# The values of two attention stages as one seven-product form, in a two-layer encoder on one core

## The chip, the cores and the metric

The kernel runs on one core of a Trainium2 chip. A core has TensorE (PE) for matmuls, VectorE (DVE), ScalarE (ACT), GpSimd (POOL) and SyncE (SP), which here only issues loads. The metric is the device time of one execution in microseconds.

## The reference

Two layers, each with a half-step SwiGLU FFN, a mixer, an attention into 256 memory tokens and a second FFN, each followed by a layer norm; 512 tokens, width 1024, float32. The even layer's mixer is another one; the change touches the odd layer's mixer and the memory attention of both layers:

```python
def mixer_c(h, w_in, w_out, rpb):        # 16 heads of 64, grid of 8 rows x 64 columns
    q, k, v = jnp.split(h @ w_in, 3, axis=-1)
    ...
    s = jnp.einsum('bwhd,bawjhd->bhwaj', q_r, k_nb).astype(jnp.float32) * scale
    s = s + bias.astype(jnp.float32)[None]
    p = jax.nn.softmax(s.reshape(B, C_HEADS, GRID_W, kh * kw), axis=-1)
    ...
    return o @ w_out

def memory_attn(h, mem, w_q, w_kv, w_o): # 4 heads of 256
    q = (h @ w_q).reshape(B, S, MEM_HEADS, MEM_HEAD_DIM)
    k, v = jnp.split(mem @ w_kv, 2, axis=-1)
    ...
    p = jax.nn.softmax(s, axis=-1).astype(v.dtype)
    o = jnp.einsum('bhsm,bmhd->bshd', p, v).reshape(B, S, D_MODEL)
    return o @ w_o
```

The values of the mixer are a product of 512 x 1024 by 1024 x 1024, those of a memory stage one of 256 x 1024 by 1024 x 1024.

## The kernel before

Every large product keeps float32 accuracy by splitting each operand into a high part (a ScalarE cast) and a low part (a VectorE subtraction, `split`, L380) and adding three matmuls, high x high, high x low, low x high (`mm3`, L391). The activations are held by features in `xh` and `xl`. The FFNs and output projections already use a seven-product form of 2 x 2 block matrices (seven block products in place of eight, paid with sums of blocks); queries, keys and values do not.

No engine order is written by hand. The program is recorded as a list of operations, all through one helper, so every row of the profile says L160. A planner (`plan`, L198) then simulates the engines with a table of costs. TensorE takes, of the operations that are ready, the one that stands first in the program; VectorE, ScalarE and GpSimd take the one with the earliest due time, worked out backwards from TensorE. The result is a fixed order for each engine. Tiles come from pools (L357): 27 `slab` buffers of 4 KB a partition, 14 `t2` of 2 KB, 2 `raw` of 8 KB, and eight PSUM banks under the tags `a`, `d` and `t`. A pool grants its buffers in the order in which the program asks, so a load on SP's queue waits until the slab it was given is free, and all loads behind it wait too.

The mixer (`mixer_c`, L1291) starts when the third FFN's layer norm ends, tile of 128 tokens by tile. It makes the values of heads 0 to 3 (group 0), the queries and keys of pair 0, the queries of pair 1 and the scores of pair 0 (`weights_of`). Then it loops over eight pairs of heads: keys of the next pair, transposes of this pair's weights (`turned`), queries two pairs on, scores of the next pair, `attend` of this pair. After `attend` of pairs 0 to 5 come two of the four token tiles of one further group of values, so that groups 1 to 3 are made inside the loop. A tile of values uses weights that stand as high and low side by side, so that a step is one matmul of 512 columns and one of 256. The pair's softmax (VectorE's reductions with the biases, ScalarE's exponentials and normalising) runs while TensorE does attend, values and keys. The biases of a pair are two table loads and six sums on GpSimd.

A memory stage (`memory`, L1484) loops over four heads; `project` makes for each the keys and two blocks of queries, and at heads 0 and 2 the values of two heads, 48 matmuls of 512, with keys and values of the 256 memory tokens. In `todo` the values stand between the keys and the queries.

Of the kernel before, what the change touches and what calls it, by code (L numbers as in the profile page):

```python
# [20 lines left out]
P = 128  # L21
D = 1024
# [314 lines left out]
class Kernel:  # L337
# [80 lines left out]

    def w_cols_k(self, w, c0):
# [154 lines left out]
    def project(self, w, ps, lo, hi):  # L574

        for k in range(KB):
            self.mm3(ps[:, lo:hi], [z[:, k, :] for z in w], self.xT(k, lo, hi), k == 0, k == KB - 1)
# [327 lines left out]
    def ffn(self, i, ln_i, last, aside=None):  # L905
# [385 lines left out]
    def mixer_c(self, ln_i, last):  # L1291
# [3 lines left out]
        ends = [self.slab(F32R, (P, KB, P)) for _ in range(2)]  # L1295

        def values(grp, t):

            if t == 0:
                wv[0] = self.w_cols_side(w_in, 2 * D + 256 * grp)  # L1300
                vp[grp] = self.slab(F32, (P, 4, 256))
                if grp == 0:
                    for dst, lo in ((slice(64, 128), 0), (slice(0, 64), 448)):
                        nc.scalar.copy(ends[0][:, :, dst], self.xh[:, :, lo : lo + 64])
                        nc.vector.tensor_copy(ends[1][:, :, dst], self.xl[:, :, lo : lo + 64])
            ps = self.ps("t" if grp else "a")
            for k in range(KB):
                x = self.xT(k, 64 + t * P, 64 + (t + 1) * P) if t < 3 else [z[:, k, :] for z in ends]
                self.side_step(ps, x, wv[0][k // 2][:, k % 2], k)
# [101 lines left out]
        def attend(pts, pair):  # L1411
            po = self.ps("d")
            for j in range(4):
                for s in range(2):
                    own = po[64 * s : 64 * s + 64]
                    dst = own[:, j * P : j * P + 256] if j < 3 else own.rearrange("p (c n) -> p c n", c=4)[:, 0:4:3]
                    c0 = 64 * (2 * (pair % 2) + s)
# [3 lines left out]
                        dst, vp[pair // 2][:, j, c0 : c0 + 64], mv, start=j == 0, stop=j == 3, skip_group_check=True  # L1421
# [14 lines left out]
        vp, qs, ks, acts = {}, {}, {}, []  # L1436
        wv, wq, wk, wo = [None], [None], [None], {}
        for t in range(NT):
            values(0, t)
# [3 lines left out]
        us = weights_of(0)  # L1443
        for pair in range(8):
# [9 lines left out]
            else:  # L1454
                steps(5 if pair == 6 else 3)
            if pair < 7:
                us = weights_of(pair + 1)
# [6 lines left out]
            if pair < 6:  # L1464
# [246 lines left out]
```

## Time and profile before

| | before |
|---|---|
| median of 3 runs | 2096.86 us (2096.57 to 2097.29) |
| profiled execution | 2095.62 us |
| its span | 2093.8 us |
| POOL busy | 307.9 us (15%) |
| first memory stage: last two key pairs and the values of heads 0, 1 | 541.69 to 553.37 us of the span |
| last output matmul of the third FFN, start of the mixer | 1363.8 us |
| scores of pairs 0, 1 and 2 of the mixer | 1399.40, 1413.97, 1435.89 us |
| DMA | 276.99 MB, mean 132 GB/s |

The page gives for each engine its busy time. For a kernel whose first engine is nearly always busy the useful question is what else is waited for, and where; that is read from the timeline of this engine, whose rows end with what ended an idle time before them, if there was one.

### The profile page before, as it was taken

How to read it: one execution, taken by the hardware profiler on the slowest of the kernel's cores; microseconds unless marked ns; L12 is line 12 of the kernel's file. 1: busy time of each engine (PE TensorE's matmuls, PEld its weight loads, DVE VectorE, ACT ScalarE, POOL GpSimd, SP SyncE). 2: the span in 40 equal slices, each digit the busy share in tenths (PEclk: the TensorE clock that was granted, in tenths of full speed). 3: DMA queues.
4: the chain of work that ended last, by engine and by line, in shares of the span. 5: the costliest groups of instructions: out<-in, count | busy, mean ns of one | idle time of the engine just before them, and what ended most of it. 6: DMA issues, size and time to landing. Idle time of an engine off the chain costs nothing.

```text
span 2093.8 us, 33128 instructions
## 1 busy us (share of the span) xinstructions
PE 2078.1 (99%) x13044; PEld 1845.2 (88%) x13044; DVE 1752.3 (84%) x2515; ACT 1146.7 (55%) x1847; POOL 307.9 (15%) x389
## 2 busy tenths in 40 slices
PE   9999999999999999999999999999999999999997
PEld 7999988777888999998899999888878889999996
DVE  7789988788748979999889999854487488799996
ACT  5555543697545744555555455446565466455552
POOL 0001005310002010000300100412131020001002
PEclk9999999999999999999999999999999999999999
DMA  7566572004343467565545657332234434556651
GB/s 209 154 158 146 139 199 86 21 21 141 122 131 101 135 144 204 142 161 143 170 114 149 158 144 201 91 106 76 100 93 141 144 98 141 130 146 170 153 148 61
DMA packets 214204, 276.99 MB, mean 132 GB/s; under 512 B 9376, under 2 KB 162592, under 8 KB 214048
## 3 DMA queue, kind: packets, MB, share of 16 engines
q1 hardware_dynamic: 177536, 217.99, 32.7%
q0 software_dynamic: 36224, 56.63, 15.5%
q8 instruction: 102, 1.67, 0.3%
q14 instruction: 54, 0.44, 0.1%
q10 hardware_dynamic: 288, 0.26, 0.0%
HBM read 272.75 MB, written 4.19 MB: 132 GB/s over the span
## 4 chain that ended last, share of the span: by engine, by line
PE 96%; DVE 2%; issue 1%; DMA 1%; ACT 0%; POOL 0%; DVEq 0%; ACTq 0%; POOLq 0%
PE a L160 53%; PE d L160 27%; PE t L160 16%; DVE slab L160 1%; DVE x L160 1%; DMA slab<-ffn_w_up 0%; DVE t L160 0%; ACT slab L160 0%; ACT t L160 0%; DMA raw<-x_t 0%; POOL rms8y L160 0%; POOL slab L160 0%; DVE xl L160 0%; DVE mn L160 0%; DVE rh L160 0%
## 5 line engine op out<-in xcount | busy, mean ns | idle before, releaser
L160 DVE TENSOR_TENSOR slab<-slab,slab 128x1024 fp32r<-128x1024 f32 (+2 forms) x617 | 734.8, 1213 | 49.0 <-ACT slab L160 42.1
L160 PE MATMUL a<-slab,slab 128*128 128x256 f32 (+3 forms) x2384 | 583.8, 317 | 0.1
L160 ACT CAST slab<-slab 128x1024 fp32r<-128x1024 f32 (+2 forms) x457 | 463.5, 1038 | 197.9 <-DVE slab L160 133.7
L160 PE MATMUL a<-raw,slab 128*128 128x256 f32 x2432 | 459.8, 283 | 0.0
L160 PEld LDWEIGHTS a<-slab,slab 128*128 128x128 f32 (+1 forms) x2384 | 415.0, 190 | 38.6 <-issue 3.6
L160 PE MATMUL a<-xh,slab 128*128 128x256 f32 (+2 forms) x2000 | 445.4, 312 | 0.2 <-ACT slab L160 0.2
L160 PEld LDWEIGHTS a<-raw,slab 128*128 128x128 f32 x2432 | 388.2, 191 | 6.2 <-ACT t L160 0.2
L160 PEld LDWEIGHTS a<-xh,slab 128*128 128x128 f32 x2000 | 333.9, 190 | 25.0 <-ACT slab L160 1.1
L160 PE MATMUL a<-xl,slab 128*128 128x256 f32 (+2 forms) x1000 | 311.8, 312 | 0.0
L160 PE MATMUL d<-slab,t 128*128 128x512 f32 x1104 | 278.9, 392 | 0.0
L160 PEld LDWEIGHTS d<-slab,t 128*128 128x128 f32 x1104 | 200.3, 189 | 36.9 <-ACT t L160 0.4
L160 PE MATMUL t<-slab,t 128*128 128x512 f32 x828 | 207.5, 392 | 0.5 <-DVE x L160 0.3
L160 PEld LDWEIGHTS a<-xl,slab 128*128 128x128 f32 x1000 | 190.4, 190 | 13.5 <-DVE xl L160 0.2
L160 PEld LDWEIGHTS t<-slab,t 128*128 128x128 f32 x828 | 150.2, 189 | 28.9 <-issue 0.7
L160 DVE TENSOR_TENSOR slab<-raw,slab 128x1024 fp32r<-128x1024 f32 (+2 forms) x144 | 158.9, 1127 | 16.5 <-ACT slab L160 16.4
L160 PE MATMUL d<-slab,slab 128*128 128x512 f32 (+3 forms) x736 | 163.3, 415 | 0.0
L160 PE MATMUL d<-xh,slab 128*128 128x256 f32 (+1 forms) x720 | 153.1, 306 | 0.0
L160 ACT CAST slab<-raw 128x1024 fp32r<-128x1024 f32 (+1 forms) x128 | 119.7, 968 | 29.3 <-DMA raw<-ab_w_in 9.6
L160 PEld LDWEIGHTS d<-slab,slab 128*128 128x128 f32 (+1 forms) x736 | 105.3, 170 | 34.3 <-issue 12.6
L160 DVE SCALAR_TENSOR_TENSOR x<-d,x 128x512 f32<-128x512 f32 x174 | 118.7, 685 | 15.8 <-PE d L160 14.0
L160 PEld LDWEIGHTS d<-xh,slab 128*128 128x128 f32 x720 | 117.1, 191 | 5.1
L160 ACT COPY t<-a 128x512 f32<-128x512 f32 (+1 forms) x112 | 62.0, 556 | 96.0 <-DVE a L160 59.4
(132 smaller groups left out, 2492.2 us busy)
## 6 DMA issues: line engine op xcount, KB each, us to landing
slab<-ffn_w_gate SPq DMA_DIRECT2D x95, 512.0 KB
slab<-ffn_w_up SPq DMA_DIRECT2D x95, 512.0 KB
slab<-ffn_w_down SPq DMA_DIRECT2D x80, 512.0 KB
slab<-ffn_w_down POOLq DMA_DIRECT2D x40, 512.0 KB, 6.4
raw<-mem_w_kv SPq DMA_DIRECT2D x16, 1024.0 KB
slab<-ffn_w_gate POOLq DMA_DIRECT2D x19, 512.0 KB, 6.1
slab<-ffn_w_up POOLq DMA_DIRECT2D x19, 512.0 KB, 6.0
raw<-mem_w_q SPq DMA_DIRECT2D x8, 1024.0 KB
```

Of the source, the lines that this page charges most:

```text
L160: op.call = lambda: fn(*args, **kw)
```

## The change

All values of the mixer become one product in seven-product form, with two token blocks of 256 (each as two tiles of 128), two halves of the contraction and two halves of the 1024 columns. With a, b, c, d the four 512 x 512 blocks of the weights (a over b on the left, c over d on the right), products 1 and 2 use a and b, product 6 uses a + c + d, product 5 c + d, product 7 a + c, product 4 d, and product 3 a + c + d + b. Products 1, 2 and 3 take the tokens' high and low parts as they are; products 6, 5, 7 and 4 take sums of token blocks, made on VectorE from a float32 copy of the normalised tokens, which the third FFN now keeps in the `raw` pool (`keep`). The sums c + d and a + c + d are made on VectorE, a + c (onto a second copy of a) and the addition of b by accumulating DMAs of GpSimd's queue.

All 14 steps (seven products, two halves of their contraction) are issued ahead of the pair loop, after the scores of pair 0; the loop has no values any more. As `raw` is taken, the first queries' and keys' weights come in four quarters into slabs (`w_pairs`). In a memory stage the same steps, with one block of 128 tokens, are drawn three, two, two, three, two and then all that are left at six points among the projections of heads 0 and 1; the memory tokens are loaded a second time in float32 for their sums.

In the whole program matmuls fall from 12916 to 12804, VectorE's TENSOR_TENSOR instructions rise from 1470 to 1508, plain loads from 408 to 428, and GpSimd's DMAs from 120 to 132.

```diff
+    def w_pairs(self, w, c0):
+        got = self.w_halves(w, c0)
+        return [[[z[i][:, :, b * P : b * P + P] for z in got] for i in range(2)] for b in range(2)]
...
+            st = [z[k // 4][:, k % 4] if isinstance(z, list) else z[:, k, :] for z in w]
+            self.mm3(ps[:, lo:hi], st, self.xT(k, lo, hi), k == 0, k == KB - 1)
...
-                ln.update({"gb": self.load_ln(ln_i), "last": last, "keep": i == 1})
+                ln.update({"gb": self.load_ln(ln_i), "last": last, "keep": i in (1, 2)})
...
-        ends = [self.slab(F32R, (P, KB, P)) for _ in range(2)]
-        def values(grp, t):
...
-            self.side_sum(vp[grp][:, t], ps)
+        def shifted(q, s):
...
+        def value_sums():
+            t1, t2, t3, t4 = (self.slab(F32, (P, 4, 256)) for _ in range(4))
+            for z, x, y, op in ((t1, (0, 0), (0, 1), ALU.subtract), (t2, (1, 1), t1, ALU.add), (t3, (0, 1), (1, 1), ALU.subtract), (t4, (1, 0), t2, ALU.subtract)):
...
+            tokens.update({5: t1, 6: t2, 7: t3, 4: t4})
+        def value_ends():
...
+        def value_prep(m):
+            if m == 6:
+                value_sums()
+            if m in tokens:
+                tokens[m] = self.wide(tokens[m])
+            if m == 3:
+                ends.extend(self.t2(F32R, (P, 4, P)) for _ in range(2))
+                value_ends()
+        def stationary(m, k, b):
+            if m == 1 or m == 2:
+                return self.xT(4 * (m == 2) + k, 64 + b * P, 64 + b * P + P)
+            if m == 3:
+                return self.xT(4 + k, 320, 448) if b == 0 else [z[:, k] for z in ends]
+            return [z[:, k, b * P : b * P + P] for z in tokens[m]]
+        def value_done(f, s, b, ps, less=None):
+            if not room[f, s]:
+                room[f, s].append(self.slab(F32, (P, 2, 512)))
+            dst = room[f, s][0][:, b]
+            if less is None:
+                nc.scalar.copy(dst, ps)
+            else:
+                self.mix(dst, ps, less, ALU.subtract)
...
-                wq[0] = self.w_cols(w_in, 128 * pair)
+                wq[0] = self.w_pairs(w_in, 128 * pair) if pair == 0 else self.w_cols(w_in, 128 * pair)
...
-                wk[0] = self.w_cols(w_in, D + 128 * pair)
+                wk[0] = self.w_pairs(w_in, D + 128 * pair) if pair == 0 else self.w_cols(w_in, D + 128 * pair)
...
-                        dst, vp[pair // 2][:, j, c0 : c0 + 64], mv, start=j == 0, stop=j == 3, skip_group_check=True
+                        dst, room[pair // 4, j // 2][0][:, j % 2, c0 : c0 + 64], mv, start=j == 0, stop=j == 3, skip_group_check=True
...
-        for t in range(NT):
-            values(0, t)
...
+        made = self.staged(self.value_steps(w_in, 2 * D, 2, value_prep, stationary, value_done))
...
         queries(0, True)
         keys(0, True)
         queries(1)
         us = weights_of(0)
+        some(99)
...
-            if pair < 6:
-                for t in range(2):
-                    values(pair // 2 + 1, 2 * (pair % 2) + t)
...
+    def value_steps(self, w, c0, blocks, ready, stationary, done):
...
+        chain = {1: ("d", 1), 2: ("d", 1), 6: ("a", 6), 7: ("a", 6), 4: ("a", 6), 5: ("d", 5), 3: ("d", 5)}
+        at = {"a": (0, 0), "b": (1, 0), "c": (0, 1), "d": (1, 1)}
...
+        def fetch(name, i):
+            z = self.slab(F32, (P, 2, 512))
+            nc.sync.dma_start(out=z, in_=part(name, i))
+            return z
+        def plus(z, name, i):
+            nc.gpsimd.dma_start(out=z, in_=part(name, i), accum_op=ALU.add)
+        def load(m, i):
+            for name in {1: "a", 2: "b", 6: "cd"}.get(m, ""):
+                raw[name, i] = fetch(name, i)
+            if m == 7:
+                raw["v", i] = fetch("a", i)
+                plus(raw["v", i], "c", i)
+        def prep(m, i):
+            if i == 0:
+                ready(m)
+            if m == 6:
+                self.mix(raw["c", i], raw["c", i], raw["d", i], ALU.add)
+                self.mix(raw["a", i], raw["a", i], raw["c", i], ALU.add)
+            right[m, i] = self.wide(raw[{1: "a", 2: "b", 6: "a", 5: "c", 7: "v", 4: "d", 3: "a"}[m], i])
+            if m == 6:
+                plus(raw["a", i], "b", i)
+        def product(m, i):
+            tag, c = chain[m]
+            for b in range(blocks):
...
+                for k in range(2):
+                    self.mm3(
+                        ps, stationary(m, 2 * i + k, b), [z[:, k] for z in right[m, i]], m == c and i == 0 and k == 0, i == 1 and k == 1,
+                        skip_group_check=True,
+                    )
+                if i == 0:
+                    continue
+                if m == 1:
+                    own["c12", b] = self.t2(F32)
+                    nc.scalar.copy(own["c12", b], ps)
+                elif m == 6:
+                    self.mix(ps, ps, own["c12", b], ALU.subtract)
+                    nc.scalar.copy(own["c12", b], ps)
+                elif m == 5:
+                    own["c22", b] = self.t2(F32)
+                    nc.scalar.copy(own["c22", b], ps)
+                elif m == 7:
+                    done(1, 1, b, ps, own["c22", b])
+                elif m == 3:
+                    done(0, 1, b, ps, own["c12", b])
+                else:
+                    done(int(m == 4), 0, b, ps)
...
+        return [tuple(bound(f, m, i) for f in (load, prep, product)) for m in (1, 2, 6, 5, 7, 4, 3) for i in range(2)]
...
+        def value_prep(m):
+            if m == 1:
+                for q in range(2):
+                    raw.append(self.slab(F32, (P, 4, MEM)))
+                    nc.sync.dma_start(out=raw[q], in_=a["mem_t"][512 * q : 512 * q + 512].rearrange("(k p) m -> p k m", p=P))
...
+            if m in sums:
+                y = self.slab(F32R, (P, 2, 4, P))
+                self.split(sums[m], y[:, 0], y[:, 1])
+                sums[m] = y
...
             def values():
-                wv = self.w_cols512(w_kv, D + 256 * head)
-                vs.extend(self.pair() for _ in range(2))
-                for m in range(2):
-                    ps = self.ps("a")
-                    for k in range(KB):
-                        self.mm3(ps, memT(k, m * P, (m + 1) * P), [z[:, k % 2, :] for z in wv[k // 2]], k == 0, k == KB - 1)
-                    for j, both in enumerate(vs):
-                        self.split(ps[:, j * 256 : j * 256 + 256], *(z[:, m * 256 : m * 256 + 256] for z in both))
+                for _ in range(rate.pop(0) if rate else 0):
+                    next(made, None)
...
-            return got, [keys] + [values] * (head % 2 == 0) + [lambda: queries(0), lambda: queries(1)]
+            return got, [keys, values, lambda: queries(0), values, lambda: queries(1), values]
...
+        rate = [3, 2, 2, 3, 2, 99]
+        made = self.staged(self.value_steps(w_kv, D, 1, value_prep, stationary, value_done))
...
-            acts += attend(p, now, hs[head] if head < 2 else None)
+            acts += attend(p, [z[:, head % 2].rearrange("p (o n) -> p (o n)", o=1) for z in room[head // 2]], hs[head] if head < 2 else None)
```

How this moves the instructions, at three places. In the pair loop, TensorE before, where `attend` of pair 0 ends (`d_2738`) and the first values of group 1 follow (`t_2746`):

```order
L160 MATMUL d_2738<-slab_2706,slab_2658 64x256
L160 MATMUL d_2738<-slab_2703,slab_2658 64x2x128
L160 MATMUL d_2738<-slab_2706,slab_2658 64x2x128
L160 MATMUL t_2746<-slab_2741,xh_83 128x512
L160 MATMUL t_2746<-slab_2741,xl_84 128x256 x2
L160 MATMUL t_2746<-slab_2741,xh_83 128x512
L160 MATMUL t_2746<-slab_2742,xl_84 128x256
L160 MATMUL t_2746<-slab_2742,xh_83 128x512
```

and TensorE now, where `attend` of the same pair (`d_2823`) ends and the keys of pair 2 follow at once (`t_2830`):

```order
L160 MATMUL d_2823<-slab_2791,slab_2785 64x256
L160 MATMUL d_2823<-slab_2788,slab_2785 64x2x128
L160 MATMUL d_2823<-slab_2791,slab_2785 64x2x128
L160 MATMUL t_2830<-xh_83,slab_2826 128x512
L160 MATMUL t_2830<-xl_84,slab_2826 128x512
L160 MATMUL t_2830<-xh_83,slab_2827 128x512
L160 MATMUL t_2830<-xh_83,slab_2826 128x512
```

The 32 matmuls of values between `attend` and the keys are gone from pairs 0 to 5.

At the head of the mixer, TensorE now, at the end of product 5 (`d_2762`) and the beginning of product 7 (banks `a_2751` and `a_2752`; `slab_2765` and `slab_2766` are the high and low of the first half of a + c, `slab_2780` the high of product 3's weights, `t_2786` the keys of pair 1):

```order
L160 MATMUL d_2762<-slab_2759,slab_2755 128x512
L160 MATMUL a_2751<-slab_2765,slab_2763 128x512
L160 MATMUL a_2752<-slab_2765,slab_2763 128x512
L160 MATMUL t_2786<-xh_83,slab_2689 128x512
L160 MATMUL t_2786<-xl_84,slab_2689 128x512
L160 MATMUL t_2786<-xh_83,slab_2690 128x512
L160 MATMUL d_2761<-slab_2780,xh_83 128x512
L160 MATMUL a_2751<-slab_2766,slab_2763 128x512
L160 MATMUL a_2751<-slab_2765,slab_2764 128x512
```

Matmuls that need only the high part come first, then three of the keys, then one of product 3, before the low of product 7 is used.

VectorE now, in the same stretch: the lows of product 4 (`slab_2774`, and `slab_2777` for its second half), of product 7 (`slab_2766`, second half `slab_2770`), of product 3 (`slab_2781`, `slab_2784`), and then the weights of the queries of pair 2 (`raw_2794`):

```order
L160 TENSOR_TENSOR slab_2774<-slab_2731,slab_2773 128x1024
L160 TENSOR_TENSOR slab_2766<-slab_2753,slab_2765 128x1024
L160 TENSOR_TENSOR slab_2781<-slab_2720,slab_2780 128x1024
L160 TENSOR_TENSOR slab_2784<-slab_2721,slab_2783 128x1024
L160 TENSOR_TENSOR slab_2777<-slab_2737,slab_2776 128x1024
L160 TENSOR_TENSOR slab_2770<-slab_2758,slab_2769 128x1024
L160 TENSOR_TENSOR slab_2796<-raw_2794,slab_2795 128x1024
L160 TENSOR_TENSOR slab_2775<-a_2751,t_2686_2767 128x512
```

The low of product 7's second half is the last of the six.

GpSimd now, from the end of the third FFN on: the additions of b onto the two halves of the sum in `slab_2720` and `slab_2721`, that of c onto the two copies of a (`slab_2753`, `slab_2758`), and the bias sums of pair 1:

```order
L160 DMA slab_2720<-c_w_in 128x2x512
L160 DMA slab_2721<-c_w_in 128x2x512
L160 DMA slab_2753<-c_w_in 128x2x512
L160 TENSOR_TENSOR t_2721_2802<-near_245,t_2720_2801 128x256 x2
L160 DMA slab_2758<-c_w_in 128x2x512
L160 TENSOR_TENSOR t_2722_2803<-near_245,t_2720_2801 128x192 x2
```

The second addition of product 7 stands behind the first two bias sums of pair 1.

More of the change, by code (lines that the diff above doesn't have):

```diff
@@ L1293, in mixer_c @@
         w_in, w_out = a["c_w_in"], a["c_w_out"]
[L1295 to L1310 removed]
+        def shifted(q, s):
+            if s == 0:
+                return [(self.xf[q][:, :, 64:256], slice(0, 192)), (self.xf[q][:, :, 256:320], slice(192, 256))]
+            return [(self.xf[q][:, :, 320:512], slice(0, 192)), (self.xf[q][:, :, 0:64], slice(192, 256))]
@@ L1455, in mixer_c @@
                 steps(5 if pair == 6 else 3)
+            if pair == 0:
+                some(99)
             if pair < 7:
@@ L1569, in memory @@
         for head in range(4):
-            p, now = weights_of(got["k"], [got["q", b] for b in range(2)]), vs.pop(0)
+            p = weights_of(got["k"], [got["q", b] for b in range(2)])
             todo = []
@@ L1576, in memory @@
             for f in todo:
-                if head == 2:
+                if head == 2 and f.__name__ != "values":
                     for _ in range(3):
```

53 lines of the change are left out of this document (45 added, 8 removed).

## The prediction

> **What bounds the kernel now.** I read the page's totals and chain first, then the timeline of TensorE where the change cuts, then windows of the engines that feed it.
>
> ```profile
> span 2093.8 us, 33128 instructions
> PE 2078.1 (99%) x13044; PEld 1845.2 (88%) x13044; DVE 1752.3 (84%) x2515; ACT 1146.7 (55%) x1847; POOL 307.9 (15%) x389
> ...
> PE 96%; DVE 2%; issue 1%; DMA 1%; ACT 0%; POOL 0%; DVEq 0%; ACTq 0%; POOLq 0%
> ```
>
> TensorE (PE) works 99% of the span and is 96% of the chain that ends last. The other engines matter only where they make it wait. So the price of an edit is the matmuls it takes away, less the waits it opens. The profiled execution took 2095.62 us, 1.8 us more than its span, and lies 1.24 us under the median of 2096.86; I sum against 2095.62 and add 1.24 at the end.
>
> **The matmuls removed.** In the first memory stage the values stand in one block of TensorE's timeline:
>
> ```profile
> 541.33 0.60 PE L160 MATMUL t<-ident,x 128*128 128x128 f32 x4
> 541.69 11.85 PE L160 MATMUL a<-slab,slab 128*128 128x256 f32 x52
> 553.37 0.28 PE L160 MATMUL a<-xh,slab 128*128 128x256 f32 x1
> ```
>
> Columns: start, busy us, engine, line, operation, tiles, shape, count. The 52 are the last two 512+256 pairs of the keys and 48 matmuls of 512 columns. From 541.69 to 553.37 are 11.68 us; with two pairs at 0.35 us (next view), (11.68 - 0.70)/48 = 0.229 us for a matmul of 512. In the mixer, around one head pair:
>
> ```profile
> 1413.97 0.96 PE L160 MATMUL a<-slab,slab 64*128 64x192 f32 x12
> ...
> 1415.53 1.95 PE L160 MATMUL d<-slab,slab 128*64 128x256 f32 x16
> 1417.41 0.50 PE L160 MATMUL t<-slab,xh 128*128 128x512 f32 x1
> ...
> 1418.33 0.40 PE L160 MATMUL t<-slab,xh 128*128 128x512 f32 x1
> ...
> 1422.88 0.40 PE L160 MATMUL t<-slab,xh 128*128 128x512 f32 x1
> 1423.11 0.39 PE L160 MATMUL t<-xh,slab 128*128 128x512 f32 x1
> ...
> 1428.57 1.04 PE L160 MATMUL t<-ident,t 128*128 128x128 f32 x8
> ...
> 1435.89 0.96 PE L160 MATMUL a<-slab,slab 64*128 64x192 f32 x12
> ```
>
> Scores, attend, values, keys, transposes, queries, then the next scores 21.92 us later. From 1418.33 to 1422.88 lie 13 pairs of 512 and 256 columns: 4.55/13 = 0.350 us a pair. The 24 key matmuls take 1428.57 - 1423.11 = 5.46, 0.2275 each.
>
> Mixer: 128 pairs go (128 x 0.350 = 44.8 us) and 7 products x 2 blocks x 4 contraction steps x 3 = 168 matmuls of 512 come (168 x 0.229 = 38.5). **-6.3 us.** Each memory stage: 96 matmuls become 7 x 4 x 3 = 84; 12 x 0.229 = 2.75, twice: **-5.5 us.** Queries, keys, scores and transposes keep their matmuls. Together -11.8 us, 0.56%.
>
> The Trainium skill, page "TensorE: Matmul & The Clock Gate", section "Back-to-back issue gap", gives about 131 ns for each sustained matmul of 512 columns and 216 ns for an isolated one. The rows show 229 ns, so the first does not hold for these matmuls. By 131 ns the memory term would be 3.1 us in place of 5.5.
>
> **What it costs VectorE (DVE).** The whole program has 42 more TENSOR_TENSOR of 1024 columns, 20 more of 512, 4 of 768 and 28 fewer of 256: the lows of the weights (14 a stage), the sums of weights and tokens, and the combining of products. Durations:
>
> ```profile
> 1375.26 2.35 DVE L160 TENSOR_TENSOR slab<-raw,slab 128x1024 fp32r<-128x1024 f32 x2
> ...
> 546.78 1.21 DVE L160 TENSOR_TENSOR slab<-raw,slab 128x1024 fp32r<-128x1024 f32 x1
> 547.92 0.68 DVE L160 TENSOR_TENSOR slab<-t,slab 128x512 fp32r<-128x512 f32 x1
> 548.54 0.42 DVE L160 TENSOR_TENSOR slab<-a,slab 128x256 fp32r<-128x256 f32 x1
> ```
>
> Back to back one of 1024 takes 1.14 us (546.78 to 547.92) and one of 512 0.62; for 256 I take 0.35, for 768 0.88. That is 48 + 12 + 4 - 10 = 54 us of VectorE, some 18 a stage. VectorE has 340 idle us in the span, but not everywhere:
>
> ```profile
> 1364.00:1374.00 10.00, 7.87 (x47) 6.15 (x46) 9.59 (x16) 4.59 (x8) 1.12 (x3) 1.00 0.01 2
> 1374.00:1413.00 39.00, 39.00 (x264) 34.76 (x263) 19.36 (x42) 18.90 (x42) 4.89 (x12) 1.00 0.45 142
> 541.70:591.70 50.00, 49.97 (x301) 44.36 (x299) 29.15 (x41) 25.62 (x47) 0.00 (x0) 1.00 0.47 148
> 591.70:640.00 48.30, 48.30 (x244) 41.05 (x243) 29.80 (x48) 27.21 (x56) 3.62 (x4) 1.00 0.48 142
> ```
>
> After the window: its length, then busy us of PE, PEld, DVE, ACT, POOL, the granted clock, DMA share, GB/s. In the first 50 us of the memory stage VectorE has 21 us free, and 18 come, nearly all in that stretch. It fits, with little over.
>
> At the **head of the mixer** it is tighter. Let T be 1363.8, where the FFN's last output matmul ends and all this begins. To T+10.2 VectorE is full with the layer norm (9.59 of 10.00). In the changed order these stand next on VectorE, up to the low of the weights of product 7's first half: about 19 of 1024 (21.7 us), five of 512 (3.1), four of 768 (3.5), six of 256 (2.1), and the ten reductions of pair 0's softmax (about 3.8). That is 34 us, so it ends at T+44; the second half comes four of 1024 later, at T+49. When does TensorE ask for them?
>
> ```profile
> 1363.76 0.39 PE L160 MATMUL a<-slab,xh 128*128 128x512 f32 x1
> ...
> 1364.93 0.39 PE L160 MATMUL a<-slab,xh 128*128 128x512 f32 x1
> 1367.36 0.39 PE L160 MATMUL a<-slab,xl 128*128 128x256 f32 x1 [2.04 <-DVE xl L160]
> ...
> 1400.96 0.50 PE L160 MATMUL t<-xh,slab 128*128 128x512 f32 x1
> ```
>
> Today the first values start at T, the scores of pair 0 end at 1400.96, T+37.2, and 32 pairs of values (11.2 us) lie between. Without them the scores end at T+26.0, or a little sooner: of the waits for the layer norm's lows (2.04 us in this row) the queries of the first two token tiles, 48 matmuls of 128 columns, may hide some. I count the waits as they are, bounds 2 us less and 0, and take T+25 as the earliest for what VectorE must meet. Then come products 1, 2, 6 and 5, 95 matmuls, 21.8 us: product 7 is due at T+46.8, and its second half 26 matmuls on, at T+52.8. VectorE arrives 3 us ahead, if it never waits itself. For what it may wait I price 0.5 us; the bounds are 0 and 6 (9 of the 34 us late).
>
> **The sums' transfers.** Products 7 and 3 need weights that GpSimd's DMA queue adds in place (part c onto a copy of a, part b onto a): four such transfers of 512 KB a stage, and 20 more plain loads on SP's queue in all.
>
> ```profile
> L160 ACT CAST slab<-slab 128x1024 fp32r<-128x1024 f32 (+2 forms) x457 | 463.5, 1038 | 197.9 <-DVE slab L160 133.7
> ...
> L160 ACT COPY t<-a 128x512 f32<-128x512 f32 (+1 forms) x112 | 62.0, 556 | 96.0 <-DVE a L160 59.4
> ...
> slab<-ffn_w_down POOLq DMA_DIRECT2D x40, 512.0 KB, 6.4
> ...
> 1404.65 2.18 POOL L160 TENSOR_TENSOR t<-near,t 128x256 f32<-128x256 f32 x4 [1.42 <-DMA t<-bias]
> ```
>
> The last row but one ends with the median from issue to landing. Counting the 27 slab buffers through the changed order, product 7's second copy of a gets its buffer when the weights of product 2 are used up, about T+33. The addition could then land by T+42. But in GpSimd's order it stands behind the first two bias sums of pair 1 (1.1 us, at 2.18/4), which wait for buffers that pair 0's reductions free, about T+42. So it lands at T+49.5, cast (1.04) and low (1.14) end at T+51.7, against T+52.8. I add 0.5 us, between 0 and 6.4.
>
> **The other edits.** Eight ScalarE copies that keep the FFN's result in float32, the split of queries' and keys' first weights in eight pieces, and the moved loads lie beside a TensorE that works through; ScalarE is busy 4.59 of 10.00 and 18.90 of 39.00 us at the head. Cost nothing; if that cover went, 8 copies of 0.556 us would be 4.4. In the memory stages the values no longer cover the 11.7 us between keys and queries, so queries come up against the low of the last token tile; I take 0.5 us a stage for it and late lows, bounds 0 and 4.
>
> **The pair loop.** Without values a period shrinks from 21.92 to 21.92 - 5.70 = 16.2 us, and the softmax of the next pair must end under attend and keys alone:
>
> ```profile
> 1414.96 0.42 DVE L160 CUSTOM_DVE_ANT_0 t<-a,t 128x256 f32<-128x256 f32 x1 [4.40 <-PE a L160]
> ...
> 1421.05 1.60 ACT L160 ACTIVATE t<-t,l 128x192 f32<-128x192 f32 x4
> ```
>
> From the scores' start (1413.97) the last normalising ends 8.7 us on (1422.65). Transposes will start after scores 1.56, attend 1.88 and keys 5.46, 8.9 us on, and the second head's four a little later. It just fits: 0, bounds 0 and 1 us a pair, six pairs.
>
> **The sum.** -11.8 + 0.5 (mixer, VectorE) + 0.5 (the addition) + 1 (two memory stages) = -9.8; 2095.62 - 9.8 = 2085.8, and with 1.24 a median of **2087 us**.
>
> **The rivals.** (a) VectorE becomes the bound at the three heads. For it: it is full for 40 us in the mixer, and it slows beside GpSimd:
>
> ```profile
> 1340.43 1.64 DVE L160 TENSOR_TENSOR slab<-raw,slab 128x512 fp32r<-128x512 f32 x1
> 1341.99 0.68 DVE L160 SCALAR_TENSOR_TENSOR x<-t,x 128x512 f32<-128x512 f32 x1
> 1342.60 0.67 DVE L160 TENSOR_TENSOR slab<-raw,slab 128x512 fp32r<-128x512 f32 x1
> ...
> 1338.53 2.99 POOL L160 TENSOR_TENSOR x<-x,slab 128x512 f32<-128x512 f32 x2
> ```
>
> A subtraction of 512 took 1.64 us while GpSimd's sums ran, and 0.67 just after. Six bias sums a pair at 0.55 us hold it up to 3.3 us in the mixer; with the 18 us of each memory stage spread unevenly, 1 to 2 us there, it is 5 to 7 us above the forecast, 2092 to 2094. Chance 0.20.
>
> The Trainium skill, "SBUF — State Buffer", section "SBUF: two separate sides", has a rule for this: a VectorE operation with two SBUF inputs and a GpSimd one that reads SBUF lock each other out of a shared port for the whole instruction. The rows agree (0.97 us lost).
>
> (b) The softmax is not covered: 1 us in each of six pairs, 2093. Against it: the 8.7 us hold work of ScalarE for the values that goes away. Chance 0.08.
>
> (c) **Slower.** The additions in place are late in all three stages, because slabs come free late and load, addition, cast and low follow one another. The load of 512 KB alone is about 1.5 us at the rates seen in 1364 to 1400:
>
> ```profile
> GB/s 0 0 0 0 0 0 0 0 0 18 0 0 0 0 0 0 67 302 387 365 312 354 362 182 0 0 166 368 398 228 97 332 382 347 40 0 0 8 196 383
> ```
>
> So the chain takes 1.5 + 6.4 + 1.04 + 1.14 = 10.1 us. If it begins only 12 matmuls (2.7 us) before product 7, TensorE waits 7.4 us, 22 in three stages, and everything in its fixed order stands behind: 2095.62 - 11.8 + 22 + 1.24 = 2107. It makes the kernel slower from 3.9 us of waiting a stage, by 0.2% from 5.3 a stage, that is where the chain begins less than 4.8 us ahead. Against it: in the mixer the buffers come free some 14 us ahead. Chance 0.10.
>
> (d) No change: the 336 new matmuls of 512 run at 0.264 us, 11.8/336 more than 0.229, since each meets new weights; 2098 at most. Against it: the 48 of the memory stage meet them too. Chance 0.07.
>
> **How the numbers follow.** My forecast, 2084.5 to 2091, has 0.55. A measurement here tells 0.2%, 4.2 us, from no change: faster means under 2092.7. Faster: 0.55, half of (a), and 0.03 of (b): 0.68. Slower, over 2101.1: (c), 0.10. The same: 0.22. The range reaches from the whole saving without a new wait (2095.62 - 11.8 + 1.24 = 2085, and 1 us of today's waits hidden: 2084) to 2098, the end of (a), (b) and (d); (c) and the forecast's edge are left out.
>
> **What would show it.** TensorE's matmul count must fall by 112. Right: product 7 of the mixer starts 46 to 49 us after the FFN's last matmul, pair periods are near 16.2 us, and the new waits sum to 2 to 3 us, named DVE slab. Wrong: waits for a slab load or an addition of over 3 us before product 7 or 3, periods above 17 us with transposes behind ACT, or 512-column matmuls further apart than 0.235 us.

## The result and the profile after

| | before | after |
|---|---|---|
| median of the first comparison | 2096.72 us (4 runs, 2096.57 to 2097.29) | 2085.40 us (4 runs, 2084.03 to 2087.97) |
| ratio, 95% interval | | 0.9945, 0.9933 to 0.9957 |
| profiled execution, span | 2095.62, 2093.8 us | 2084.03, 2082.1 us |

The kernel became 11.3 us faster, 0.55%. The page's totals after, engine by engine (busy us, share of the span, instructions), and the shares of the chain that ended last:

```profile
span 2082.1 us, 33087 instructions
PE 2065.3 (99%) x12932; PEld 1832.4 (88%) x12932; DVE 1806.3 (87%) x2553; ACT 1175.8 (56%) x1869; POOL 325.0 (16%) x401
...
PE 93%; issue 3%; DVE 2%; DMA 1%; POOL 1%; ACT 0%; DVEq 0%; POOLq 0%; ACTq 0%; SPq 0%
```

TensorE has 112 matmuls fewer (13044 to 12932; the profile shows 128 more in both kernels than the counts of the program given above), VectorE 54.0 us more (1752.3 to 1806.3). TensorE is still the bound, with 99% of the span, and its share of the chain falls from 96% to 93%; so what counts is how much of its removed work came back as idle time. Windows of the first memory stage, the mixer and the second memory stage answer that; each window runs between the same two matmuls of both programs, to within about 0.1 us. Columns: length, then busy us of PE, PEld, DVE, ACT and POOL, the granted clock, DMA share, GB/s. Before:

```profile
540.50:623.70 83.20, 83.17 (x466) 72.50 (x466) 44.88 (x65) 38.32 (x74) 1.28 (x1) 1.00 0.47 146
1363.76:1591.55 227.79, 225.65 (x1384) 186.75 (x1382) 139.99 (x313) 133.42 (x319) 47.62 (x91) 1.00 0.30 93
1591.55:1680.95 89.40, 89.37 (x507) 78.00 (x506) 51.71 (x74) 44.88 (x85) 3.55 (x3) 1.00 0.48 154
```

After:

```profile
540.60:620.70 80.10, 80.10 (x455) 70.05 (x454) 61.63 (x82) 46.69 (x83) 5.59 (x5) 1.00 0.56 165
1360.78:1583.73 222.95, 219.35 (x1296) 179.18 (x1295) 159.90 (x314) 146.23 (x326) 60.00 (x106) 1.00 0.38 110
1583.73:1670.00 86.27, 86.27 (x494) 75.52 (x493) 68.70 (x93) 52.38 (x93) 8.53 (x7) 1.00 0.59 177
```

Length against PE busy shows the whole result. The memory stages lose 3.10 and 3.13 us and are as full as they were, with VectorE at 61.63 of 80.10 us. The mixer's matmuls lose 225.65 - 219.35 = 6.30 us, but the stage loses only 4.84: TensorE's idle time in it rises from 2.14 to 3.60 us. The three stages give 11.07 of the span's 11.7 us; the other 0.6 us lie in smaller pieces elsewhere.

The idle times of TensorE by waiting tile and releaser (total us, times, longest), before:

```profile
PE a L160 <- DVE xl L160: 2.0, 1, 2.0
...
PE t L160 <- DVE x L160: 0.3, 1, 0.3
```

and after:

```profile
PE d L160 <- ACT slab L160: 2.6, 1, 2.6
PE t L160 <- DVE junk L160: 1.2, 1, 1.2
PE d L160 <- DVE x L160: 1.0, 1, 1.0
PE t L160 <- POOL slab L160: 0.6, 1, 0.6
```

The wait for the layer norm's low parts (`xl`, 2.0) is gone; new are 2.6 us for a `slab` of ScalarE and 1.0 us for `x` of VectorE. DVE junk and POOL slab stand in both kernels, outside the three stages. The timeline of after shows where the new ones are; the number in brackets is the idle time just before. TensorE:

```profile
1360.78 0.22 PE L160 MATMUL a<-xh,slab 128*128 128x128 f32 x1
...
1366.09 0.62 PE L160 MATMUL t<-ident,x 128*128 128x128 f32 x4
...
1405.79 0.62 PE L160 MATMUL a<-slab,slab 128*128 128x512 f32 x2
...
1406.69 0.39 PE L160 MATMUL t<-xh,slab 128*128 128x512 f32 x1
1409.65 0.50 PE L160 MATMUL d<-slab,xh 128*128 128x512 f32 x1 [2.57 <-ACT slab L160]
...
1437.82 0.96 PE L160 MATMUL a<-slab,slab 64*128 64x192 f32 x12
...
1454.23 0.96 PE L160 MATMUL a<-slab,slab 64*128 64x192 f32 x12
...
1555.97 1.20 PE L160 MATMUL d<-slab,t 128*128 128x512 f32 x4 [1.03 <-DVE x L160]
```

The mixer starts at T = 1360.78. Matmuls of 128 columns, the queries of the first tokens, run from T to 1366.09 without a gap: they cover the old layer norm wait. Product 7 starts at 1405.79, T + 45.0, and one product 3 matmul, moved ahead of product 7's low parts, waits 2.57 us. The pair loop has no wait and a period of 1454.23 - 1437.82 = 16.41 us. The last row is a wait in the mixer's output projection.

What the product 3 matmul waits for is a cast on ScalarE. GpSimd, VectorE and ScalarE at that place:

```profile
1402.87 1.19 POOL L160 DMA_DIRECT2D slab<-c_w_in  x1 [5.82 <-DMA slab<-c_w_in]
...
1403.65 4.39 POOL L160 TENSOR_TENSOR t<-near,t 128x192 f32<-128x192 f32 x4
...
1403.94 3.74 DVE L160 TENSOR_TENSOR slab<-slab,slab 128x1024 fp32r<-128x1024 f32 x2
1409.63 3.61 DVE L160 TENSOR_TENSOR slab<-slab,slab 128x1024 fp32r<-128x1024 f32 x3 [1.95 <-ACT slab L160]
...
1408.07 0.59 ACT L160 COPY t<-d 128x512 f32<-128x512 f32 x1 [3.40 <-POOL t L160]
1408.55 1.99 ACT L160 CAST slab<-slab 128x1024 fp32r<-128x1024 f32 x2
```

ScalarE stands still for 3.40 us before `COPY t<-d`, which moves the result of product 5 (the program's `c22`) out of PSUM into a `t2` buffer. The pool gave it the buffer that had held a bias table of pair 1, so it must wait until GpSimd's bias sums have read it; and these four sums take 4.39 us. (The program asks for the copy's tile, `t_2686_2767`, before that table, `t_2720_2801`; but in the planned order the table's load comes first. So here the buffer was handed out in the planned order, not in that of the program, as was said above of the pools.) Behind the copy, in ScalarE's fixed order, stand the casts of product 3's weights, though their data are there. The first of them ends at 1409.60, and TensorE goes on.

VectorE has no lead at this place either. The second subtraction of its row of two is the low of product 7's first half; it ends at 1407.68. After the matmul at 1406.69 two more, at 0.23 us each, would have brought TensorE to that low at about 1407.15, by an estimate from the spacing of these rows. So without ScalarE's wait TensorE would still have stood about 0.5 us for VectorE; some 2 of the 2.57 us are the buffer's. VectorE itself then stands 1.95 us for the late casts.

### The profile page after: what moved, and what is told of

It is laid out like the page before. It is cut to its first block, busy times and chain, and to the rows that moved or that the text cites. A ratio compares the mean times of both kernels' runs of the same rounds, so it can differ in the third digit from the quotient of the medians.

```text
span 2082.1 us, 33087 instructions
## 1 busy us (share of the span) xinstructions
PE 2065.3 (99%) x12932; PEld 1832.4 (88%) x12932; DVE 1806.3 (87%) x2553; ACT 1175.8 (56%) x1869; POOL 325.0 (16%) x401
## 4 chain that ended last, share of the span: by engine, by line
PE 93%; issue 3%; DVE 2%; DMA 1%; POOL 1%; ACT 0%; DVEq 0%; POOLq 0%; ACTq 0%; SPq 0%
PE a L160 51%; PE d L160 28%; PE t L160 14%; DVE slab L160 1%; DVE x L160 1%; DMA slab<-ffn_w_up 0%; DVE t L160 0%; DMA slab<-c_w_in 0%; ACT slab L160 0%; POOL slab L160 0%; POOL t L160 0%; ACT t L160 0%; DMA raw<-x_t 0%; POOL rms8y L160 0%; DVE mn L160 0%
## 5 line engine op out<-in xcount | busy, mean ns | idle before, releaser
L160 DVE TENSOR_TENSOR slab<-slab,slab 128x1024 fp32r<-128x1024 f32 (+3 forms) x693 | 820.7, 1207 | 50.5 <-ACT slab L160 39.3
L160 ACT CAST slab<-slab 128x1024 fp32r<-128x1024 f32 (+2 forms) x515 | 519.9, 1033 | 206.2 <-DVE slab L160 141.5
L160 PE MATMUL a<-slab,slab 128*128 128x256 f32 (+3 forms) x2320 | 571.2, 316 | 0.0
L160 PEld LDWEIGHTS a<-slab,slab 128*128 128x128 f32 (+1 forms) x2320 | 403.6, 190 | 36.1 <-issue 3.6
L160 PEld LDWEIGHTS a<-xl,slab 128*128 128x128 f32 x1000 | 190.3, 190 | 13.7 <-DVE xl L160 0.3
L160 PE MATMUL d<-slab,slab 128*128 128x512 f32 (+3 forms) x856 | 194.0, 412 | 0.0
L160 PEld LDWEIGHTS d<-slab,slab 128*128 128x128 f32 (+1 forms) x856 | 127.0, 173 | 39.1 <-issue 12.3
L160 DVE TENSOR_TENSOR slab<-raw,slab 128x1024 fp32r<-128x1024 f32 (+3 forms) x112 | 127.0, 1153 | 5.6 <-ACT slab L160 5.4
L160 PE MATMUL d<-xl,slab 128*128 128x256 f32 (+1 forms) x360 | 109.7, 305 | 0.0
```

The source lines that it names most:

```text
L160: op.call = lambda: fn(*args, **kw)
```

## The experiments

The theory after the trace: the mixer's loss is this borrowed buffer, through ScalarE's order. The rival is the prediction's own: VectorE is late, and ScalarE's wait only hides it. The times below are medians; each ratio is against the kernel before, run in the same comparison (2096.41 to 2096.93 us).

**The change again**, without an edit (`e1_again`, five rounds; a third series, `e10_changed_third`, below).

> The changed kernel once more, for its spread. Its four times went from 2084.03 to 2087.97 us, those of before only from 2096.57 to 2097.29. Theory W (one wait in the mixer's head, ScalarE standing still for a buffer, is the only new wait and it depends on when transfers land): the profile shows again one wait of 2 to 4 us before the first matmul of product 3, named ACT slab, and no other over 1.3 us; median 2084 to 2087. Rival V (VectorE is the bound at three heads): waits at all three heads, named DVE slab.

Measured 2085.91 us (2084.18 to 2086.07), ratio 0.9948 (0.9936 to 0.9961). The wait before product 3 is there again, 2.56 us, and this time something follows it. The same ten matmuls behind it in the timeline, first in after, then in this execution:

```profile
1409.98 2.48 PE L160 MATMUL a<-slab,slab 128*128 128x512 f32 x10
```

```profile
1409.74 0.50 PE L160 MATMUL d<-slab,xh 128*128 128x512 f32 x1 [2.56 <-ACT slab L160]
1410.08 4.04 PE L160 MATMUL a<-slab,slab 128*128 128x512 f32 x10
```

They take 4.04 in place of 2.48 us. The window of these 3 us shows why, in its third number from the end, the granted clock:

```profile
1410.00:1413.00 3.00, 3.00 (x9) 2.34 (x9) 2.98 (x3) 3.00 (x6) 0.00 (x0) 0.56 0.04 8
```

In after it is 1.00 there, here 0.56: so in this execution the wait cost 2.6 us and then 1.6 more.

**The mixer alone** (`e2_mixer_only`) and **the memory stages alone** (`e3_memory_only`). The first keeps the change but has `memory` as it was, the second the reverse:

```diff
-            return got, [keys, values, lambda: queries(0), values, lambda: queries(1), values]
+            return got, [keys] + [values] * (head % 2 == 0) + [lambda: queries(0), lambda: queries(1)]
```

> Only the mixer changed, the memory stages as before. From the aligned traces the mixer gave 4.8 us: 2091.9 us, ratio 0.9977, and the spread of about 4 us stays with it, if the spread comes from the wait before product 3. If the parts depend on each other through the plan, it is off by over 2 us.

> Only the two memory stages changed, the mixer as before. From the aligned traces they gave 3.1 us each: 2090.5 us, ratio 0.9970, with a spread as small as that of before (under 1 us). By my forecast (12 matmuls less, 0.5 us of waits) 2.25 each: 2092.2. If VectorE were the bound at the memory heads, waits named DVE slab of 1 us and more there.

Mixer alone: 2092.53 us (11 runs, 2090.42 to 2095.08), ratio 0.9983 (0.9974 to 0.9991), 3.9 us gained. Memory alone: 2091.01 us (7 runs, 2089.30 to 2092.82), ratio 0.9973 (0.9962 to 0.9984), 5.4 us gained. The sum, 9.3, is near the 10.5 of the whole in the same comparison. The mixer alone has the wait before product 3 too, so it doesn't come from the memory stages; memory alone has the old wait for `xl`:

```profile
PE d L160 <- ACT slab L160: 2.5, 1, 2.5
...
PE d L160 <- DVE x L160: 1.0, 1, 1.0
```

```profile
PE a L160 <- DVE xl L160: 2.0, 1, 2.0
```

I had expected the memory kernel to scatter little, as it has no wait that could let the clock fall; its runs spread over 3.5 us all the same. So that wait isn't the only source of the spread, and the other stays open.

**Another buffer for the copy** (`e4_c22_slab`). The result of product 5 goes into a slab; the wait for GpSimd goes with the buffer, and nothing else is edited:

```diff
-                    own["c22", b] = self.t2(F32)
+                    if b == 0:
+                        c22 = self.slab(F32, (P, 2, 512))
+                        for j in range(2):
+                            own["c22", j] = c22[:, j]
```

> The copy of product 5 goes into a slab in place of a t2 buffer. Theory W: ScalarE no longer stands 3.4 us behind pair 1's bias sums, the wait of 2.57 us before product 3 falls under 0.7 us, and the kernel is 2.0 to 2.6 us faster than the changed one, 2082.8 to 2083.4 on its profile, ratio 0.9930 to 0.9936, with a smaller spread. Rival V (the low parts on VectorE are as late): the wait stays at 1.5 us or more, now named DVE slab, gain under 1 us. Rival T (the additions land late): the wait moves to product 7's second half, named ACT slab or a DMA, gain under 1 us.

Measured 2082.68 us (2081.66 to 2085.54), ratio 0.9937 (0.9924 to 0.9951): 3.2 us under the change in the same comparison, though the two intervals overlap. Between the two profiled executions, 2086.07 and 2082.68, lie 3.4 us: 1.7 are waits, 1.6 the fall of the clock in e1. The spread, which I had expected to shrink, did not: 3.9 us, against 1.9 in e1. ScalarE now goes through the place without standing still:

```profile
1405.67 0.57 ACT L160 COPY slab<-d 128x512 f32<-128x512 f32 x1
1406.14 2.00 ACT L160 CAST slab<-slab 128x1024 fp32r<-128x1024 f32 x2
1408.04 0.58 ACT L160 COPY slab<-d 128x512 f32<-128x512 f32 x1
```

The copy starts 2.4 us earlier than in after, and the wait before product 3 is gone. One wait of 0.87 us has come at the head of the mixer, before the second half of product 7, where rival T had put it: GpSimd issues that addition at 1408.99, 6 us later than in after. So the wait before product 3 hangs on the copy's buffer. The run doesn't take the buffer alone away, though: the planner also put pair 1's bias sums earlier, where the last ends at 1397.87, and VectorE's subtractions before product 7, no longer beside them, take 1.23 us each in place of 1.87. The 0.5 us that VectorE would have cost went with that.

**The bias sums later** (`e5_bias_late`). The other way to free the copy: GpSimd makes pair 1's biases only after the last addition of product 7, so the copy no longer gets a buffer that they hold.

```diff
+            nc.after = (self.added, ("gpsimd",)) if pair == 1 else None
             tables, q, k = biases(pair), qs.pop(pair), ks.pop(pair)
+            nc.after = None
...
                 plus(raw["v", i], "c", i)
+                self.added = nc.ops[-1]
```

> Pair 1's bias tables and sums may start only behind the last addition of product 7; everything else as changed. They are then out of the way three times: the copy of product 5 no longer gets the table's buffer, the sums no longer meet VectorE's subtractions, and the addition is issued at once. Theory W: no wait of over 0.7 us is left between the third FFN and the pair loop; 2.6 us less than the changed kernel without the clock's fall, up to 4 with it: 2082 to 2083, ratio 0.9930 to 0.9935; VectorE's two subtractions that took 3.74 us take 2.3. Rival V (VectorE late anyway): a wait of 1 us or more named DVE slab before product 7 or 3; gain under 1.5 us.

Measured 2083.77 us (2083.40 to 2085.66), ratio 0.9940 (0.9928 to 0.9953). The wait before product 3 is gone here too, and VectorE's subtractions no longer meet GpSimd's sums: four of 1024 columns take 4.63 us, 1.16 each, against 1.87 each in the row of after above. But one wait of over 0.7 us is left, against the expectation.

```profile
1406.49 4.63 DVE L160 TENSOR_TENSOR slab<-slab,slab 128x1024 fp32r<-128x1024 f32 x4 [1.12 <-ACT slab L160]
...
1408.71 1.19 POOL L160 DMA_DIRECT2D slab<-c_w_in  x1 [12.59 <-DMA slab<-c_w_in]
...
1415.08 4.04 POOL L160 TENSOR_TENSOR t<-near,t 128x192 f32<-128x192 f32 x4 [4.02 <-DMA t<-bias]
...
1414.60 1.04 ACT L160 CAST slab<-slab 128x1024 fp32r<-128x1024 f32 x1 [1.53 <-DMA slab<-c_w_in]
...
1415.70 0.73 PE L160 MATMUL a<-slab,slab 128*128 128x512 f32 x2 [1.01 <-ACT slab L160]
```

What is late now is product 7's second addition: it is issued only at 1408.71, after 12.59 us of waiting for the plain load that it adds onto, and TensorE waits 1.01 us for the cast behind it. In SP's order that load stands behind the 1024 KB load of the next queries' weights (issued at 1395.40 and 1394.49); in after it stands ahead of it.

**More work for VectorE** (`e7_dup_lows`). If VectorE were the bound, 4.6 us more of it (four subtractions, 1.16 each) would come back as waiting. The kernel of e5, with the low parts of products 6 and 5 computed twice in the mixer:

```diff
+            if blocks == 2 and m in (6, 5):
+                hi, lo = right[m, i]
+                nc.vector.tensor_tensor(out=lo, in0=raw[{6: "a", 5: "c"}[m], i], in1=hi.bitcast(F32), op=ALU.subtract)
```

> As e5, with the low parts of the weights of products 6 and 5 in the mixer computed twice: four subtractions of 1024 more on VectorE, 4.6 us, before product 7. By my forecast VectorE is 3 us ahead there, so TensorE waits 1.5 to 2 us more than in e5. If VectorE has just no slack, 4 to 4.6 us more. If it has 5 us and more, nothing.

Measured 2081.64 us (2080.88 to 2083.01), ratio 0.9928 (0.9915 to 0.9942): with more work it has the lowest median of all kernels, though the intervals of e4, e6 and e11 overlap with its own, and TensorE has no wait at the head of the mixer. VectorE there, up to product 7:

```profile
1392.83 7.34 DVE L160 TENSOR_TENSOR slab<-slab,slab 128x1024 fp32r<-128x1024 f32 x6
...
1407.06 5.89 DVE L160 TENSOR_TENSOR slab<-slab,slab 128x1024 fp32r<-128x1024 f32 x5 [0.62 <-ACT slab L160]
1412.86 0.42 DVE L160 CUSTOM_DVE_ANT_0 t<-t,t 128x256 f32<-128x256 f32 x1
```

The planner, with other costs to weigh, put six of pair 0's eight softmax reductions (the custom rows) behind the weights' lows, where nothing waits for them yet, and in SP's order it put the load for product 7 ahead of the queries' weights: the addition is issued 10 us sooner than in e5.

```profile
1398.48 1.19 POOL L160 DMA_DIRECT2D slab<-c_w_in  x1 [2.69 <-DMA slab<-c_w_in]
```

So the gain over e5 isn't from the doubled work but from the order that came with it. What the run tells apart: 4.6 us more of VectorE's work fit in ahead of product 7 once six reductions (about 2 us) stand behind it and GpSimd's sums elsewhere. So the amount of VectorE's work isn't the bound at this place, and the rival falls in that form. The run doesn't show slack in the order of the changed kernel, where the low came about 0.5 us late.

**The steps of the memory stages in one block** (`e8_memory_block`). All 14 steps stand between the keys and the queries of head 0, in place of three, two, two, three, two and the rest:

```diff
-        rate = [3, 2, 2, 3, 2, 99]
+        rate = [99]
```

> As changed, but in the memory stages all steps of the values are drawn at one point, between the keys and the queries of head 0, and none later. VectorE has then some 18 us of work more ahead of the first queries, and TensorE only 19 us of products to meet it. By the forecast's ledger VectorE ends 5 to 9 us behind TensorE there: waits named DVE slab or ACT slab of 3 to 8 us a stage, 6 to 16 us slower than changed, about 2092 to 2101. If VectorE were far from full, no change.

Measured 2113.11 us (2111.97 to 2114.45), ratio 1.0076 (1.0060 to 1.0091), 27 us over the change, where I had expected 6 to 16 over it. The matmuls are the same; the waits of TensorE, in the whole execution, are not:

```profile
PE d L160 <- ACT slab L160: 8.8, 3, 4.4
PE a L160 <- ACT slab L160: 5.5, 5, 2.2
PE a L160 <- DVE slab L160: 3.8, 4, 1.4
```

The first row holds 2.8 us of the mixer's old wait; those of the two memory stages come to 7.2 and 8.9 us, about the most that I had expected. A part of each stage in windows:

```profile
560.00:580.00 20.00, 16.36 (x75) 14.03 (x76) 17.06 (x21) 12.40 (x16) 0.00 (x0) 0.83 0.39 95
1610.00:1620.00 10.00, 4.26 (x19) 2.68 (x17) 10.00 (x12) 6.68 (x10) 3.46 (x4) 0.77 0.68 190
```

What I hadn't priced is the granted clock, 0.83 and 0.77 here: TensorE's busy time rises from 2065.3 us in after to 2079.0 with the same matmuls. These 13.7 us and the 16.1 of waits make up nearly all of the 30.4 us between the two profiled executions.

A step needs a cast (1.04 us) and a low (1.14 to 1.16 us) of 1024 columns for six matmuls, 1.4 us of TensorE, and VectorE makes sums besides; drawn one behind another, products outrun their weights. VectorE is busy 10.00 of 10.00 us in the second window, while TensorE has 4.26, and ScalarE's next casts stand 1.98 us for its sums there (at 1616.46). So here, in one block, VectorE does hold TensorE up, as in the prediction's rival (a). Additions come late as well (two are issued at 1615.54, after 11.92 us of waiting for a load); how the two share the waits, no run tells apart. The spread order is what keeps these stages free of waits, and without it the seven products would have been a loss.

**The memory tokens earlier.** The last wait of the mixer, 1.03 us for `x` in the output projection, has VectorE making lows of the second memory stage's tokens (`memory_tokens`, called at pair 6) while GpSimd adds. In after:

```profile
1551.77 2.98 POOL L160 TENSOR_TENSOR x<-x,slab 128x512 f32<-128x512 f32 x2 [1.77 <-DVE l L160]
...
1552.27 3.04 DVE L160 TENSOR_TENSOR slab<-raw,slab 128x512 fp32r<-128x512 f32 x2
```

Two lows of 512 columns take 3.04 us there. `e9_tokens_4` is the change with this call at pair 4, `e6_bias_late_tokens_4` the same on the kernel of e5; `e11_best_again` repeats the latter and `e10_changed_third` the change.

```diff
-            if pair == 6:
+            if pair == 4:
                 self.memory_tokens()
```

> The changed kernel with the memory tokens loaded and split after pair 4 in place of pair 6, and nothing else. If the second new wait (1.03 us for VectorE's sum into x) comes from these subtractions, it falls under 0.4 us and the one before product 3 stays at about 2.6: some 1.0 us less than changed, 2084.5 us median. If it is VectorE's backlog from the shorter pairs, it stays at 0.7 or more.

> As e5, and the memory tokens are loaded and split after pair 4 in place of pair 6. The changed kernel has a second new wait, 1.03 us at 1555.97 for VectorE's sum into x, behind two subtractions for the memory tokens that took 3.04 us beside GpSimd's sums. If these are its cause, the wait goes: 1.0 us less than e5. If it is VectorE's own backlog from the shorter pairs, 0.7 us or more of it stays.

> The changed kernel a third time, beside e9 and e11 on one chip. Median 2085 to 2086; the wait before product 3 again near 2.6 us. If TensorE's clock falls after that wait, as in e1 and e2 but not in the first profile, its profile is near 2086, if not near 2084.

> The kernel of e6 again, beside the changed one: both new waits gone, 3 to 4 us less than the changed one, 2081 to 2083, ratio to before 0.9925 to 0.9935.

| | median | runs from, to | ratio, interval |
|---|---|---|---|
| e10, the change | 2085.83 us | 2085.52, 2086.43 | 0.9947, 0.9933 to 0.9960 |
| e9, tokens at pair 4 | 2084.60 us | 2083.53, 2086.29 | 0.9941, 0.9929 to 0.9954 |
| e6, and biases late | 2082.22 us | 2080.24, 2084.79 | 0.9930, 0.9918 to 0.9943 |
| e11, the same again | 2083.41 us | 2081.02, 2084.24 | 0.9932, 0.9920 to 0.9945 |

The waits of e9:

```profile
PE d L160 <- ACT slab L160: 2.5, 1, 2.5
PE t L160 <- ACT t L160: 1.3, 2, 0.7
```

The wait for `x` is gone, but one of 0.7 us for ScalarE has come at nearly the same place (1553.1 us), so the move gains a few tenths in the trace. That is too little to tell in the times of e9 and e10. In the profile of e6 the second half of product 7 doesn't wait; in that of e11, the same program, it waits 1.15 us for a cast, against the expectation, since the addition is issued 1.06 us later (1407.87 against 1406.81): this kernel stands on the edge. Which of e4, e6 and e7 is best, the intervals don't tell.

## Why the prediction was right

The time came out where the prediction put it, 2085.4 against 2087, within its range. Its mechanism, matmuls taken away less the waits that open, held; where the waits would come from it had wrong, and that they sum up so well is partly luck. By its own terms:

**The matmuls.** Mixer -6.3: measured 6.30 in TensorE's busy time. Each memory stage -2.75: 3.07 and 3.10 in the windows. Right, the second a little too small.

**VectorE's work.** Forecast 54 us more, some 18 a stage: measured 54.0, in the three windows 16.8, 19.9 and 17.0.

**"0.5 us a stage" for late lows in the memory stages.** Nothing came: both windows are filled by matmuls to within 0.01 us. The e8 run shows why: the draws spread over six points. With the previous term this makes -6.2 for the two stages in place of -4.5, most of what the forecast lacks against the profiled execution (2084.03 against 2085.8).

**"I count the waits as they are"**, for the layer norm's lows. Too cautious: the 128-column queries hid the whole 2.04 us, the far bound of that term. This is also why product 7 starts at T + 45.0, before the 46 to 49 us that I had named as the sign.

**The mixer's two half-microseconds, VectorE and the addition.** Here the size was off and the cause was wrong. The waits new in the mixer are 2.57 + 1.03 = 3.6 us, and with the 2.04 hidden the net is +1.5 (by the windows), where I had +1.0: two errors that nearly cancel, which is luck. The step that failed is the ledger of VectorE, "VectorE arrives 3 us ahead", as the place to look. It put product 7's low at T+44 (with ten softmax reductions ahead of it, where the trace has eight and two reciprocals); in after it ended at T+46.9, a slowing beside GpSimd included (3.74 us for the two subtractions, where 2.35 stood in the rows of before), about 0.5 us after TensorE would have come to it. That wait stayed hidden behind a longer one of which the prediction says nothing: it never asked what ScalarE's copies of products out of PSUM wait for. For ScalarE it priced eight other copies, at nothing, because ScalarE is busy half the time; but an engine that is half idle still stands still when the first instruction in its order lacks a buffer. I had named "DVE slab" as the new waits' releaser; they are ACT slab and DVE x. The second one wasn't in the prediction at all.

**The addition** I put at T + 49.5 for landing. In after it is issued at 1402.87, T + 42.1, and there its half of product 7 doesn't wait. In e4, e5 and e11 it is issued at 1408.99, 1408.71 and 1407.87, 5 to 6 us later, as the plain load that it adds onto lands later, and that half waits 0.87, 1.01 and 1.15 us. So the term is real where the load is late, about twice the 0.5 us of the forecast and far from rival (c). Whether it would show in after without the wait before product 3, no run tells.

**The pair loop.** Predicted 16.2 us and covered: 16.41, with no wait. Rival (b) is out.

**The rivals.** (a), 5 to 7 us of waits for VectorE, didn't come about: the memory stages have none, and in the mixer VectorE would have cost about 0.5 us. But e8 shows that it does where the steps stand in one block. One part of (a) was right, the slowing of VectorE beside GpSimd: 1.87 us for a subtraction that takes 1.16 in e5. It was just not what TensorE waited for last. (c) didn't happen here. (d) is out by the busy time.

## What to carry to other kernels

When a change adds a copy out of PSUM, ask which buffer of a shared pool it will be granted and who still reads it, and then what stands behind the copy on its engine: here a table's buffer, read by GpSimd, held up casts that had nothing to do with it, for 2.6 us. A ledger of the engine that feeds TensorE shows only whether its work fits; the order on a half-idle engine needs its own reading. A product whose operands need preparing is best drawn in steps among work that is ready: in this kernel the spread was worth 27 us, waits and the fall of the clock together, more than twice the whole gain.

## What the hardware showed

Six executions have the wait of 2.5 to 2.8 us before product 3 with the change's mixer (after, e1, e2, e8, e9, e10). In four of them (e1, e2, e8, e10) the granted clock falls to about half (0.50 to 0.56) for 3 us right behind it, in two it stays at 1.00. The windows, of e9 and then of e10 and e2:

```profile
1410.00:1413.00 3.00, 3.00 (x14) 2.42 (x14) 2.98 (x3) 3.00 (x6) 0.00 (x0) 1.00 0.09 16
```

```profile
1410.00:1413.00 3.00, 2.97 (x7) 2.39 (x8) 2.98 (x3) 3.00 (x5) 0.00 (x0) 0.50 0.06 12
```

```profile
1412.40:1415.40 3.00, 2.94 (x7) 2.36 (x8) 2.94 (x3) 3.00 (x6) 0.00 (x0) 0.50 0.18 31
```

Seven matmuls in place of 14 in the same 3 us: the wait costs about 1.5 us more. The Trainium skill, page "TensorE: Matmul & The Clock Gate", section "Why this matters for your kernels", advises no idle gaps of TensorE over about 3 us, as one idle window brings the clock to 4/8. The size of the fall agrees; the length doesn't quite, since here it followed waits of 2.48 to 2.77 us in four executions of six. What decides between the two outcomes the runs don't show.
